# Storing the pieces of the feed-forward way up: another order of differences and stores, and seven staging tiles in place of five

## The chip, the cores and the metric

The kernel runs on one core of a Trainium2 chip. The metric is the device time of one execution in microseconds. It is float32 work throughout; products on TensorE are made from split operands (a high part and the rest, both in the fp32r type).

## The reference, cut to what matters

The whole is one step of a decoder layer: a mixer, a cross-attention over a memory, and a feed-forward part, for 1024 prompt rows and 8 sample rows. The change lies in the feed-forward part alone:

```python
def ffn(x, g, w1, w2):
    h = rmsnorm(x, g) @ w1
    return jnp.square(jax.nn.relu(h)) @ w2
...
    xp = xp + ffn(xp, g_ffn[l], ffn_w1[l], ffn_w2[l])
```

`w1` is 1024 x 4096 and `w2` is 4096 x 1024. Prompt and sample rows stand together as N = 1032 columns of a transposed activation.

## The kernel before, in words

Both feed-forward products are made by a seven-product scheme for 2 x 2 blocks (Strassen's, in Winograd's form). Each matrix is cut into 2 x 2 blocks, seven products of sums and differences of blocks replace eight, and VectorE (DVE) and GpSimd (POOL) make the sums.

**The way up** (`up_unit`, L2049 on) makes the squared-ReLU hidden activation `h`, 256 hidden columns (a *pair*) at a time. There are 16 pairs. The first two (pairs 0 and 1, tiles `hpl`) are made by plain products while the cross-attention ends; the other 14 are *units* 0 to 13, and unit n makes pair n + 2. A unit has eight steps, A11, S2, S1, A12, S3, S4, A21, A22 in this order (i = 0 to 7), and 132 matmuls (a window of one unit also counts the one that crosses its edge): A11, A12 and A22 have 24, the others 12. Their results lie in the banks `fa` to `fg` and `fe`. Three evacuations matter below. ScalarE (ACT) copies the half-made bank `fa` into `gc` after A11, and A12 may only go on adding into `fa` after that (`gc<-fa`). DVE reads the half-made bank `fd` after S3 (`hc<-fd`), and A22 may only go on adding into it after that. Each weight operand of a product is split into a high part (ACT) and a rest (DVE), both named `wop`, five products ahead (`prep`, `LOOK = 5`).

**What is stored.** The way down needs, of each pair, its four blocks and their differences as operands: B11, T1, B22, T3, T2, B21, T4. The four blocks a, b, c, d are the halves (516 columns) of the two `hc` tiles, and `h_done` makes the differences in place: b - a into a's room (T1), d - b into b's (T3), then d - T1 into d's (T2), and c - T2 into c's (T4). Each store (`h_store`, L1952 to L1965) takes a staging tile, writes the high part into it on ACT and the rest on DVE (`halves`), and issues a DMA from SP to the DRAM tensors `hd`. A pair thus has seven stores and four differences: eleven *pieces*. The pieces of pairs 0 and 1 wait in the list `slow`; those of a unit's own pair stand in `early` (put into the program at the start of its step A22) and `rest` (appended to `bg`, taken by `bg_run` in the next unit).

**What sets the order.** The lines of `up_unit` say in which order pieces are emitted, through two tables: how many pieces of `bg` go with each step, and at which steps one of `slow` goes:

```python
            bg_run((2, 1, 1, 3, 1, 0, 0, 0)[i])
            if i in (0, 6) and slow:
                slow.pop(0)()
```

A scheduler then sets each engine's own order from priorities and its idea of when things are ready. Once set, every engine, and SP's list of DMAs too, runs strictly in that order, so an instruction that waits holds up all that stand behind it on its engine.

**Staging tiles.** `ST["ring"]` holds the staging tiles: two halves of `hst`, a part of `wsum`, `MKV`, and from unit 1 a fifth made of two `hst` halves that are stored by two DMAs (L1964). Stores take them in turn. For the last pair only the first two are used, and for the one before it three, because the others' rooms are wanted.

**The way down** follows (`down_unit`): its first operands, B11 and T2 of the first two pairs, are read back into two tiles `hfirst` (`h_load`), whose rooms are taken in the last unit but one (n == 12): one is a `q` slot, one an `e` slot. In the kernel before, the `q` slot that it gets is the one that pair 0's tile `hpl` leaves.

Of the kernel before, what the change touches and what calls it, by code (L numbers as in the profile page):

```python
# [24 lines left out]
N = NP + NS  # L25
# [27 lines left out]
def trunk_step(ctx: ExitStack, tc: tile.TileContext, I: dict, O: list):  # L53
# [17 lines left out]
    def T(tag, w, name, dt=F32):  # L71

        n = SLOTS[tag][1]
        if tag in slots and cur[0] is main:
            pump(lambda: slots[tag])
            assert slots[tag], (tag, name)
            slots[tag].remove(min(slots[tag]))
        return big.tile([128, SLOTS[tag][0]], dt, tag=tag, bufs=n, name=name)[:, :w]

    def v3(ap, a):  # L80
        return ap.rearrange("p (a b) -> p a b", a=a)
# [21 lines left out]
    @contextmanager  # L103
    def lift(n):

        tc.cur_priority -= n
        lifted[0] += n
        yield
        tc.cur_priority += n
        lifted[0] -= n  # L110
# [48 lines left out]
    def act(out, in_, func, **kw):  # L159
        spend("act", 190 + 0.72 * size(in_))  # L160
        if func not in (AF.Ln, AF.Tanh):
            return ACT.activation(out, in_, func, **kw)  # L162
        if func != table["func"]:
            follow(ACT.preload_act_table_set(TABLES[func]).ins)
            table["func"] = func
        ins = ACT.activation(out, in_, func, **kw)
        follow(ins.ins)
        return ins

    def tt(out, a, b, op):  # L170
        spend("dve", 62 + 1.04 * size(out))
        return DVE.tensor_tensor(out, a, b, op=op)  # L172
# [23 lines left out]
    def f32r(ap):  # L196
        return ap.bitcast(F32R)
# [173 lines left out]
    def halves(hi, lo, src):  # L371

        act(hi, src, AF.Copy)
        tt(lo, src, f32(hi), SUB)
# [72 lines left out]
    def bg_run(n):  # L447
        for _ in range(min(n, len(bg))):
            bg.pop(0)()
# [1153 lines left out]
    for tag in "ddee":  # L1603
        p = T(tag, 2048, "x")
# [255 lines left out]
    A11, S2, S1, A12, S3, S4, A21, A22 = range(8)  # L1860
    B11, T2, B21, T1, T3, B22, T4, GA = range(8)
    NPAIR, NPLAIN, NUNIT = DFF // 256, 2, DFF // 512
    HALF, QU, NOP = N // 2, N // 4, 7

    def F(tag, w, name, dt=F32):
        return big.tile([128, SLOTS[tag][0]], dt, tag=tag, bufs=SLOTS[tag][1], name=name)[:, :w]
# [7 lines left out]
    ST, HC, PL = {}, {}, {}  # L1874
# [47 lines left out]
    def prep(q):  # L1922

        if q >= len(QUEUE):
            return
        n, i = QUEUE[q]
        with lift(LIFT_W):
            k = q - BASE[n]
            if k == 0:
                unit_sums(n)  # L1930
            elif k < 5 and n + 1 < len(UNITS):
                unit_raw(n + 1, (k - 1,))
            t = F("wh" if q % 2 else "wl", 1024, "wop", F32R)
            src = SUM[n][i]
            k = src.shape[1]
            hi, lo = v3(t[:, :512], k), v3(t[:, 512:], k)
            halves(hi, lo, src)
            OPS[q] = hi, lo

    def terms(ps, ops, xs, first, last):  # L1940

        n = len(ops)
        for j, ((wh, wl), (xh, xl)) in enumerate(zip(ops, xs)):
            mm(ps, wh, xh, start=first and j == 0, stop=False, skip_group_check=True)
            mm(ps, wh, xl, start=False, stop=False, skip_group_check=True)
            mm(ps, wl, xh, start=False, stop=last and j == n - 1, skip_group_check=True)

    def square_relu(o, x):
        act(o, x, AF.Relu)
        act(o, o, AF.Square)  # L1950

    def h_store(p, op, src):  # L1952

        ring_ = ST["ring"][:{NPAIR - 1: 2, NPAIR - 2: 3}.get(p)]
        st = ring_[ST["n"] % len(ring_)]
        ST["n"] += 1
        hi, lo = (f32r(x) for x in st[:2])
        halves(hi, lo, src)
        d = hd[p // 2].rearrange("(s o) p (q c) -> o p s q c", s=2, q=2)[op, :, :, p % 2]
        if len(st) > 2:  # L1960
            SP.dma_start(d, v3(st[2], 2))
        else:
            for k in range(2):
                SP.dma_start(d[:, k], st[k])  # L1964

    def h_done(p, h):


        def st(op, src):
            return lambda: h_store(p, op, src)  # L1970

        def sub(o, a, b):
            return lambda: tt(o, a, b, SUB)

        a, b, c, d = (x[:, i * HALF:(i + 1) * HALF] for x in h for i in range(2))
        return ([st(B11, a), sub(a, b, a), st(T1, a)],
                [sub(b, d, b), st(T3, b), st(B22, d), sub(d, d, a), st(T2, d), st(B21, c), sub(c, c, d), st(T4, c)])

    def pl_cell(f, g, b):

# [64 lines left out]
    def up_unit(n):  # L2045
        p = UNITS[n][1]
        h = {(f, g): HC["h"][3 * f + g] for f in range(2) for g in range(3)}
        p1, U, V = HC["g"][:3]
        ps = {}  # L2049

        def bank(f, name):
            ps[name] = f(name)[:, :GW]
            return ps[name]

        for i in range(8):
            q = 8 * n + i
            prep(q + LOOK)
            bg_run((2, 1, 1, 3, 1, 0, 0, 0)[i])
            if i in (0, 6) and slow:
                slow.pop(0)()  # L2060
            if i == A22:
                early, rest = h_done(p, HC["t"])
                for fn in early:
                    fn()
            hi, lo = OPS.pop(q)
            w = [(hi[:, k], lo[:, k]) for k in range(4)]
            if i == A11:
                terms(bank(psA, "fa"), w, XOP[B11], True, False)
                with lift(LIFT_E):
                    act(p1, ps["fa"], AF.Copy)  # L2070
                terms(bank(psB, "fe"), w, XOP[GA][:4], True, False)
            elif i == A12:
                terms(ps["fa"], w, XOP[B21], False, True)
                terms(ps["fe"], w, XOP[GA][4:], False, True)
                with lift(LIFT_E):
                    square_relu(h[0, 0], ps["fa"])
                    square_relu(h[0, 2], ps["fe"])
            elif i == S2:
                terms(bank(psD, "fb"), w, XOP[T2], True, True)
                with lift(LIFT_E):  # L2080
                    tt(U, ps["fb"], p1, ADD)
            elif i == S1:
                terms(bank(psD, "fc"), w, XOP[T1], True, True)
                with lift(LIFT_E):
                    tt(V, ps["fc"], U, ADD)
            elif i == S3:
                terms(bank(psC, "fd"), w, XOP[T3], True, False)
                with lift(LIFT_E):
                    tt(h[1, 1], ps["fd"], V, ADD)
                act(h[1, 1], h[1, 1], AF.Relu)  # L2090
                act(h[1, 1], h[1, 1], AF.Square)
            elif i == S4:
                terms(bank(psD, "fg"), w, XOP[B22], True, True)
                with lift(LIFT_E):
                    tt(h[0, 1], ps["fg"], V, ADD)
                act(h[0, 1], h[0, 1], AF.Relu)
                act(h[0, 1], h[0, 1], AF.Square)
            elif i == A21:
                terms(bank(psB, "fe"), w, XOP[GA][:4], True, False)
            else:  # L2100
                terms(ps["fd"], w, XOP[T4], False, True)
                terms(ps["fe"], w, XOP[GA][4:], False, True)
                with lift(LIFT_E):
                    tt(h[1, 0], ps["fd"], U, ADD)
                    square_relu(h[1, 2], ps["fe"])
                act(h[1, 0], h[1, 0], AF.Relu)
                act(h[1, 0], h[1, 0], AF.Square)
            if n == 1 and i == A11:
                ST["ring"].append([F("ws", HALF, "hst") for _ in range(2)])
            if n == NPAIR - NPLAIN - 2:  # L2110

                if i == S2:
                    for op, tag in ((B11, "q"), (T2, "e")):
                        t = F(tag, 2 * N, "hfirst")
                        HOP["r", op] = [v3(t[:, j * N:(j + 1) * N], 2) for j in range(2)]
                elif i in (A12, A21):
                    h_load(0, B11 if i == A12 else T2)
            if n == NPAIR - NPLAIN - 1:

                for op in {S1: (B21, T1), S4: (T3,), A21: (B22,)}.get(i, ()):  # L2120
                    h_load(0, op)
        bg.extend(rest)
# [181 lines left out]
    def w1_blk(f):  # L2304
        return wcols("ffn_w1", [(0, 128 * f, 128)])
# [29 lines left out]
    slow, loads = [], {}  # L2335
# [20 lines left out]
    a, b, c, d, e, f, g = (w1_blk(i) for i in (0, 1, 2, 0, 3, 1, 2))  # L2356
# [28 lines left out]
    for c in range(1, NUNIT):  # L2385
        for op in range(NOP):
            n, k = divmod(2 * op + 1, NOP)
# [44 lines left out]
```

## Time and profile before

| what | us |
|---|---|
| median of 3 runs | 1395.52 |
| lowest of 3 runs | 1391.74 |
| the profiled execution, its own time | 1388.7 |
| its span in the profile | 1387.0 |
| unit 0 of the way up begins | 745.92 |
| the way down begins | 1047.53 |

The span runs from the first to the last instruction of the profile; the 1.7 us between it and the execution's own time lie around it. Engines are PE (TensorE matmuls), DVE (VectorE), ACT (ScalarE), POOL (GpSimd) and SP, whose queue issues the DMAs. A row of the timeline gives start, duration, engine, line, operation, output<-input, and in brackets how long its engine sat idle before it and what ended that. Idle time of an engine that nothing waits for costs nothing.

### The profile page before, as it was taken

Reading aid. Unit: us, or ns where it says so; the run is one execution under the profiler, and the core shown is the slowest. Engines: PE = TensorE matmul, PEld = TensorE weight load, DVE = VectorE, ACT = ScalarE, POOL = GpSimd, SP = SyncE. Lnnn points to the kernel's source line nnn. Section 1 sums busy time; section 2 is a strip of 40 time slices with the busy share of each in tenths; the row PEclk is TensorE's granted clock in tenths of the full one; section 3 lists DMA queues with packets and bytes.
Section 4 is the critical chain, followed back from the end, with each engine's and each line's share of the span. In section 5 each row is a group of like instructions: output and inputs, shape, how many; then the busy total and the mean of one; then the engine's idle time right before and its main releaser. Section 6 shows DMA issues by size and latency. Waiting matters only on the chain.

```text
span 1387.0 us, 24759 instructions
## 1 busy us (share of the span) xinstructions
PE 1320.7 (95%) x9251; PEld 1214.8 (88%) x9251; DVE 1026.6 (74%) x2044; ACT 683.7 (49%) x1399; POOL 263.7 (19%) x245
## 2 busy tenths in 40 slices
PE   6999999999997889998999999999999999999998
PEld 4899888777876877786789999998998999999998
DVE  6276787668767764667699888878877687877785
ACT  5265455245476555555566666756666322222222
POOL 3001011300003101011004322313231333212310
PEclk9999999999999899999899999999999999999999
DMA  6114010211101544442232677776859979776624
GB/s 186 46 49 122 9 49 18 67 25 31 47 9 40 153 131 143 130 140 77 71 123 94 229 255 250 267 255 219 298 200 346 392 271 344 258 244 205 238 72 123
DMA packets 181759, 215.89 MB, mean 156 GB/s; under 512 B 28114, under 2 KB 116238, under 8 KB 181624
## 3 DMA queue, kind: packets, MB, share of 16 engines
q1 hardware_dynamic: 181000, 214.02, 46.4%
q8 instruction: 73, 1.20, 0.4%
q0 software_dynamic: 640, 0.30, 0.1%
q14 instruction: 46, 0.38, 0.1%
HBM read 145.28 MB, written 70.06 MB: 155 GB/s over the span
## 4 chain that ended last, share of the span: by engine, by line
PE 61%; DVE 18%; ACT 9%; DMA 6%; issue 5%; SPq 1%; POOL 0%; DVEq 0%; ACTq 0%; POOLq 0%
PE win L142 9%; PE c L142 7%; PE d L142 7%; PE a L142 6%; PE wo L142 6%; PE b L142 3%; PE v L142 3%; DMA hd<-hst 2%; ACT hc L162 2%; DVE hst L172 2%; DVE hc L172 2%; PE gx L142 2%; PE f L142 2%; DMA hd<-wsum 1%; DVE wop L172 1%
## 5 line engine op out<-in xcount | busy, mean ns | idle before, releaser
L1919 POOL TENSOR_TENSOR wsum<-wraw 128x512 f32<-128x512 f32 x60 | 88.5, 1476 | 402.2 <-DMA wraw<-in_ffn_w_dram 189.2
L142 PE MATMUL win<-XL,wh 128*128 128x344 f32 x384 | 127.4, 332 | 0.0
L142 PE MATMUL win<-XH,wh 128*128 128x344 f32 x384 | 126.8, 330 | 0.2 <-ACT xy L162 0.2
L142 PE MATMUL win<-XH,wl 128*128 128x344 f32 x384 | 126.1, 328 | 0.0
L162 ACT ACTIVATE wh<-ws 128x512 fp32r<-128x512 f32 x130 | 80.0, 627 | 74.6 <-DMA ws<-in_w_out_dram 22.4
L142 PE MATMUL fe<-XH,wop 128*128 128x344 f32 x448 | 114.9, 320 | 0.0
L172 DVE TENSOR_TENSOR wl<-ws,wh 128x512 fp32r<-128x512 f32 x130 | 93.3, 730 | 26.8 <-ACT wh L162 22.1
L162 ACT ACTIVATE wop<-wsum 128x512 fp32r<-128x512 f32 x104 | 65.1, 626 | 97.3 <-PE d L142 29.1
L162 ACT ACTIVATE wop<-wraw 128x512 fp32r<-128x512 f32 x104 | 64.1, 625 | 93.2 <-PE a L142 30.4
L172 DVE TENSOR_TENSOR wop<-wsum,wop 128x512 fp32r<-128x512 f32 x104 | 88.0, 847 | 25.8 <-ACT wop L162 25.4
L172 DVE TENSOR_TENSOR wop<-wraw,wop 128x512 fp32r<-128x512 f32 x104 | 75.9, 729 | 14.1 <-ACT wop L162 13.2
L142 PEld LDWEIGHTS fe<-XH,wop 128*128 128x128 f32 x448 | 78.9, 188 | 0.0
L142 PEld LDWEIGHTS win<-XL,wh 128*128 128x128 f32 x384 | 72.7, 189 | 5.2 <-issue 3.9
L142 PEld LDWEIGHTS win<-XH,wl 128*128 128x128 f32 x384 | 72.8, 190 | 3.6 <-issue 2.7
L142 PEld LDWEIGHTS win<-XH,wh 128*128 128x128 f32 x384 | 72.8, 190 | 3.3 <-issue 1.9
L142 PE MATMUL fe<-XL,wop 128*128 128x344 f32 x224 | 71.5, 319 | 0.0
L142 PE MATMUL d<-XH,wop 128*128 128x258 f32 x352 | 67.3, 283 | 0.0
L172 DVE TENSOR_TENSOR hst<-hc,hst 128x516 fp32r<-128x516 f32 x63 | 55.7, 891 | 15.6 <-ACT hst L162 15.3
L142 PE MATMUL wo<-XH,wh 128*128 128x344 f32 x192 | 64.3, 335 | 2.0 <-ACT wh L162 2.0
L142 PE MATMUL wo<-XH,wl 128*128 128x344 f32 x192 | 64.2, 334 | 1.0 <-DVE wl L172 0.9
L162 ACT ACTIVATE hc<-hc 128x344 f32<-128x344 f32 x126 | 61.1, 485 | 4.9 <-DVE hc L172 3.2
L162 ACT ACTIVATE hst<-hc 128x516 fp32r<-128x516 f32 x63 | 39.6, 634 | 48.1 <-DVE hc L172 35.5
(551 smaller groups left out, 4143.4 us busy)
## 6 DMA issues: line engine op xcount, KB each, us to landing
wraw<-in_ffn_w_dram SPq DMA_DIRECT2D x120, 256.0 KB
hd<-hst SPq DMA_DIRECT2D x52, 516.0 KB
XH<-hd SPq DMA_DIRECT2D x34, 516.0 KB
XL<-hd SPq DMA_DIRECT2D x34, 516.0 KB
hd<-wsum SPq DMA_DIRECT2D x23, 516.0 KB
xoph<-hd SPq DMA_DIRECT2D x20, 516.0 KB
xopl<-hd SPq DMA_DIRECT2D x20, 516.0 KB
hd<-MKV SPq DMA_DIRECT2D x19, 516.0 KB
```

The lines of the kernel that those rows point to most:

```text
L142: PE.matmul(out, lhsT, rhs, start=start, stop=stop, **kw)
L162: return ACT.activation(out, in_, func, **kw)
L172: return DVE.tensor_tensor(out, a, b, op=op)
L1919: POOL.tensor_tensor(o, a, b, op=op)
```

## The change

It edits four places.

- `h_done`: the store of T1 goes from `early` to `rest`, behind the difference d - b; T3's store goes behind the difference that makes T2. The pieces of a pair are the same eleven.
- `up_unit`: with step A11 three pieces of `bg` are emitted in place of two, and the pieces of `slow` go with steps A21 and A22 (i = 6, 7) in place of A11 and A21 (0, 6).
- `up_unit`: at unit 6's step A11 two more staging tiles are added, the halves of one `q` slot.
- `h_store`: pair 13 uses the first five staging tiles only, so that the new ones are free for `hfirst`.

```diff
@@ h_store @@
-        ring_ = ST["ring"][:{NPAIR - 1: 2, NPAIR - 2: 3}.get(p)]
+        ring_ = ST["ring"][:{NPAIR - 1: 2, NPAIR - 2: 3, NPAIR - 3: 5}.get(p)]
@@ h_done @@
-        return ([st(B11, a), sub(a, b, a), st(T1, a)],
-                [sub(b, d, b), st(T3, b), st(B22, d), sub(d, d, a), st(T2, d), st(B21, c), sub(c, c, d), st(T4, c)])
+        return ([st(B11, a), sub(a, b, a)],
+                [sub(b, d, b), st(T1, a), st(B22, d), sub(d, d, a), st(T3, b), st(T2, d), st(B21, c), sub(c, c, d), st(T4, c)])
@@ up_unit @@
-            bg_run((2, 1, 1, 3, 1, 0, 0, 0)[i])
-            if i in (0, 6) and slow:
+            bg_run((3, 1, 1, 3, 1, 0, 0, 0)[i])
+            if i in (6, 7) and slow:
                 slow.pop(0)()
@@ up_unit @@
             if n == 1 and i == A11:
                 ST["ring"].append([F("ws", HALF, "hst") for _ in range(2)])
+            if n == 6 and i == A11:
+
+                t = F("q", 2 * N, "hst")
+                ST["ring"] += [(x[:, :HALF], x[:, HALF:], x) for x in (t[:, :N], t[:, N:])]
```

TensorE's own order does not change. Two places of the other engines' orders are shown.

The first is ACT in unit 7 of the way up, from the evacuation of `fe` after A12 to the first evacuation of A22's results. `hpl` is a plain pair's tile; `hc_7328` holds blocks a and b, `hc_7329` c and d; rows that write `hst`, `wsum_7330` or `MKV` from `hc` or `hpl` are the high parts of stores. Before:

```order
L162 ACTIVATE hc_7328<-fe_8955 128x344
L162 ACTIVATE wop_9050<-wsum_7330 128x512
L162 ACTIVATE hc_7328<-hc_7328 128x344
L162 ACTIVATE wop_9073<-wsum_7330 128x512
L162 ACTIVATE hc_7329<-hc_7329 128x344 x2
L162 ACTIVATE wsum_7330<-hpl_6855 128x516
L162 ACTIVATE wop_9093<-wraw_7212 128x512
L162 ACTIVATE hc_7328<-hc_7328 128x344 x2
L162 ACTIVATE hst_7647<-hc_7328 128x516
L162 ACTIVATE wop_9113<-wsum_7330 128x512
L162 ACTIVATE hst_7331<-hc_7328 128x516
L162 ACTIVATE hc_7329<-hc_7329 128x344 x2
```

The same stretch in the changed kernel, from the evacuation of S3's bank on:

```order
L162 ACTIVATE hc_7329<-hc_7329 128x344 x2
L162 ACTIVATE wop_9092<-wraw_7212 128x512
L162 ACTIVATE hc_7328<-hc_7328 128x344 x2
L162 ACTIVATE MKV_124<-hc_7328 128x516
L162 ACTIVATE wop_9112<-wsum_7330 128x512
L162 ACTIVATE hst_7644<-hc_7328 128x516
L162 ACTIVATE hc_7329<-hc_7329 128x344 x2
```

and, right behind it, up to the next unit's `gc<-fa`:

```order
L162 ACTIVATE hst_7331<-hc_7329 128x516
L162 ACTIVATE hc_7329<-fe_9098 128x344
L162 ACTIVATE wop_9151<-wsum_7330 128x512
L162 ACTIVATE hc_7329<-hc_7329 128x344
L162 ACTIVATE MKV_124<-hpl_6855 128x516
L162 ACTIVATE gc_6996<-fa_9162 128x344
```

The plain pair's store has gone from between the evacuations of S3 and S4 (one stands just ahead of `gc<-fa` now). The store of T1 (`hst_7331<-hc_7328` before, `hst_7644<-hc_7328` now) has kept its place between the `wop` and the evacuation of A22.

The second place is SP's list of DMAs around `hfirst`, the room that the way down's first B11 is read into (hd0 holds pairs 0 and 1, hd3 pairs 6 and 7, hd6 pairs 12 and 13). Before, in unit 5:

```order
L1961 DMA hd0_4481<-wsum_7330 128x2x516
L1961 DMA hd3_4484<-hst_7331 128x2x516
L2139 DMA hfirst_10084<-hd0_4481 128x1032
L1961 DMA hd3_4484<-MKV_124 128x2x516
L1961 DMA hd3_4484<-hst_7331 128x2x516
```

Now, in unit 11:

```order
L1908 DMA wraw_7366<-in_ffn_w1_dram 128x2x256 x3
L1961 DMA hd6_4487<-hst_8749 128x2x516
L2143 DMA hfirst_10081<-hd0_4481 128x1032 x2
L1961 DMA hd6_4487<-hst_7331 128x2x516
L1961 DMA hd6_4487<-wsum_7330 128x2x516
```

The two loads have moved six units later and stand right behind the last store out of the new staging tiles (`hst_8749`), whose slot they fill.

## Rows read from the trace of the kernel before

**Rows 1.** The page: busy time of each engine, its share of the span, instructions.

```profile
PE 1320.7 (95%) x9251; PEld 1214.8 (88%) x9251; DVE 1026.6 (74%) x2044; ACT 683.7 (49%) x1399; POOL 263.7 (19%) x245
```

**Rows 2.** Windows, units 3, 4, 5, 8, 9, 10, 13, way down's start: length, busy times, clock, DMA.

```profile
808.26:829.04 20.78, 20.78 (x133) 20.78 (x133) 16.87 (x24) 14.43 (x29) 5.96 (x5) 1.00 0.76 259
829.04:850.57 21.53, 21.12 (x134) 20.75 (x134) 18.00 (x25) 13.24 (x27) 6.05 (x5) 1.00 0.66 237
850.57:873.22 22.65, 21.33 (x133) 20.72 (x133) 19.80 (x29) 15.63 (x32) 5.97 (x4) 1.00 0.80 276
...
914.78:937.97 23.19, 21.28 (x133) 20.74 (x133) 19.18 (x28) 14.61 (x30) 6.18 (x4) 1.00 0.67 236
937.97:962.18 24.21, 21.40 (x134) 20.71 (x133) 20.14 (x29) 16.30 (x33) 6.24 (x4) 1.00 0.66 234
962.18:983.56 21.38, 21.03 (x133) 20.77 (x133) 17.54 (x25) 14.28 (x29) 7.70 (x5) 1.00 0.75 259
...
1025.12:1047.53 22.41, 21.30 (x133) 20.76 (x133) 18.03 (x26) 13.62 (x28) 6.68 (x4) 1.00 0.70 246
1047.53:1061.73 14.20, 12.23 (x100) 11.82 (x99) 11.39 (x12) 8.83 (x19) 6.20 (x4) 1.00 0.97 358
```

**Rows 3.** Timeline of PE: its longer idle stretches in units 5, 8 and 9.

```profile
869.36 0.40 PE L142 MATMUL fd<-XH,wop 128*128 128x344 f32 x1 [1.23 <-DVE hc L172]
...
923.99 0.42 PE L142 MATMUL fa<-XH,wop 128*128 128x344 f32 x1 [1.50 <-ACT gc L162]
...
946.78 0.42 PE L142 MATMUL fa<-XH,wop 128*128 128x344 f32 x1 [1.11 <-ACT gc L162]
...
958.32 0.40 PE L142 MATMUL fd<-XH,wop 128*128 128x344 f32 x1 [1.70 <-DVE hc L172]
```

**Rows 4.** Timeline of ACT: stores that waited, and two evacuations of `fa`.

```profile
866.18 0.64 ACT L162 ACTIVATE hst<-hc 128x516 fp32r<-128x516 f32 x1 [1.81 <-DMA hd<-hst]
...
904.51 0.64 ACT L162 ACTIVATE wsum<-hc 128x516 fp32r<-128x516 f32 x1
...
913.53 0.64 ACT L162 ACTIVATE wsum<-hpl 128x516 fp32r<-128x516 f32 x1 [3.12 <-DMA hd<-wsum]
...
920.15 0.64 ACT L162 ACTIVATE hst<-hc 128x516 fp32r<-128x516 f32 x1 [3.36 <-DVE hc L172]
...
923.50 0.44 ACT L162 ACTIVATE gc<-fa 128x344 f32<-128x344 f32 x1
...
935.17 0.64 ACT L162 ACTIVATE hst<-hpl 128x516 fp32r<-128x516 f32 x1 [1.97 <-DMA hd<-hst]
...
954.66 0.64 ACT L162 ACTIVATE hst<-hc 128x516 fp32r<-128x516 f32 x1 [2.41 <-DMA hd<-hst]
...
976.02 0.64 ACT L162 ACTIVATE MKV<-hpl 128x516 fp32r<-128x516 f32 x1 [1.70 <-DMA hd<-MKV]
...
1006.53 0.64 ACT L162 ACTIVATE wsum<-hc 128x516 fp32r<-128x516 f32 x1 [3.64 <-DVE hc L172]
...
1032.40 0.44 ACT L162 ACTIVATE gc<-fa 128x344 f32<-128x344 f32 x1
```

**Rows 5.** Timeline of DVE in unit 8's beginning.

```profile
914.20 0.69 DVE L172 TENSOR_TENSOR wsum<-hpl,wsum 128x516 fp32r<-128x516 f32 x1 [3.81 <-ACT wsum L162]
914.82 1.78 DVE L172 TENSOR_TENSOR wop<-wraw,wop 128x512 fp32r<-128x512 f32 x1
...
919.43 0.68 DVE L172 TENSOR_TENSOR hc<-hc 128x516 f32<-128x516 f32 x1
```

**Rows 6.** ACT's waits from 740 to 1070 us: in total, times, longest.

```profile
ACT hst L162 <- DVE hc L172: 35.3, 25, 3.6
...
ACT hst L162 <- DMA hd<-hst: 17.2, 13, 2.5
```

**Rows 7.** Chain that ended last: a store, from its issue to its landing.

```profile
909.05 4.46 DMA hd<-wsum
```

**Rows 8.** Timeline of SP's queue in unit 5.

```profile
859.05 0.33 SPq L2139 DMA_DIRECT2D hfirst<-hd  x1
```

## The prediction

> **What bounds the kernel now.** I read the page's first lines, then windows of one unit each, then the timelines of PE, ACT and DVE around PE's idle stretches, then ACT's waits. TensorE is busy for 1320.7 us [rows 1] of the span's 1387.0, so only its gaps can be won, and the change touches those of the way up and the hand-over to the way down alone.
>
> The reader is to see in the windows that a unit without a gap takes 20.78 us and PE is busy throughout (unit 3 [rows 2]). Eight of the 14 units are of that kind. The other six last 21.53, 22.65, 23.19, 24.21, 21.38 and 22.41 us [rows 2], so they are over the floor by 0.75 (unit 4), 1.87 (5), 2.41 (8), 3.43 (9), 0.60 (10) and 1.63 us (13): 10.69 us together. The way down's first window is 14.20 us with 12.23 us of PE, which is 1.97 us more. The clock is 1.00 in all of them. So 12.66 us is all that this change can win: 0.9% of the time.
>
> PE's named releasers are ACT's `gc<-fa` and DVE's `hc<-fd` [rows 3]. Neither is slow in itself; both engines stand in order behind a store that waits for its staging tile. Unit 8 shows the chain. ACT waits 3.12 us at 913.53 for the DMA that still reads the tile `wsum`, to put a plain pair's piece in it [rows 4]. DVE, whose next row is the rest of that piece, stands for 3.81 us; then its next `wop` takes 1.78 us, and the difference b - a starts at 919.43 only [rows 5]. ACT has meanwhile gone on to T1's store and waits 3.36 us for this difference until 920.15; `gc<-fa` starts at 923.50 [rows 4], and PE, which wanted that bank, stands 1.50 us before 923.99 [rows 3]. In unit 9 the plain pair's store at 935.17 (1.97 us of waiting, just before the unit) leads to the 1.11 us at 946.78 and T4's store at 954.66 (2.41 us) to the 1.70 us at 958.32; in unit 5 T4's store at 866.18 (1.81 us) leads to 1.23 us [rows 3, 4].
>
> ACT waits for store DMAs 17.2 us on `hst` alone, and for differences on DVE 35.3 us there [rows 6]. The second figure is larger, but most of it comes with no gap of PE: in unit 12, for one, T1's store waits 3.64 us at 1006.53 [rows 4], and the unit keeps the floor.
>
> **The change part by part.**
>
> *Two more staging tiles.* Fourteen pairs' seven stores and 14 of the plain pairs are 112, or 8 a unit. With five tiles a tile's turn comes every 5/8 of 20.78 us, or 13.0 us; with seven, 18.2 us. What a tile needs shows on `wsum`: written at 904.51, issued at 909.05, landed 4.46 us later, free at 913.53: 9.0 us [rows 4, 7]. Five tiles leave 4.0 us for bunching, and the pieces are bunched; seven leave 9.2 us. So I take the DMA waits of units 7 to 12 as gone: 3.12, 1.97, 2.41 and 1.70 us of ACT [rows 4], and the gaps behind them. Of unit 8's 2.41 I count 2.0 (the 0.4 left comes from a difference), of unit 9's 3.43 all, of unit 10's all 0.6 (its wait is the one at 976.02): 6.0 us. The bounds are 0 and 6.44.
>
> *The plain pairs' pieces at A21 and A22.* ACT's order shows what this does: the store that stood between the evacuations of S3 and S4, where A22 waits for DVE, now stands ahead of `gc<-fa`. That helps units 4 and 5, where there are still five tiles. Unit 4's gap follows such a store; I count 0.4 of its 0.75. In unit 5 the two loads into `hfirst`, the first of them at 859.05 [rows 8], also leave for unit 11. I count half of its 1.87, or 0.9. The bounds for the two units are 0 and 2.62.
> It costs something in front of `gc<-fa`: one store of 0.64 us [rows 4] more in the units that get one there. In unit 13, where T1's wait was long, `gc<-fa` started at 1032.40 [rows 4], 7.28 us after the unit's start; PE wants the bank after 48 of 132 matmuls, 7.56 us. So the room is 0.3 us in a late unit, and some 0.3 us is lost in each of perhaps three units: 1.0 us, with bounds of 0 and 2.
>
> *T1 behind another difference.* The order says that this does little on ACT: T1's store stands where it stood, straight behind the next `wop` and ahead of A22's evacuation. The 3.36 us kind of wait stays. B22's store, which needs no difference, now comes ahead of T3's, so T3's wait shrinks; neither ended a gap by itself, so I count 0, with bounds of -1 and +1. As many instructions run as before; the work hides below PE's, as DVE is busy for 16.87 to 20.14 us of a unit [rows 2].
>
> *Five to seven, and back.* Where the count changes at unit 6, the fifth tile gets T1 and, two stores later, T3 of the same pair: 2/8 of 20.78 is 5.2 us, against 9.0 needed: up to 3.8 us of ACT. A wait of 2.41 us made a gap of 1.70 and one of 1.81 a gap of 1.23 [rows 3, 4], so a gap is about 0.6 to 0.7 shorter than the wait, and this one at most 3.1 us. But the tile is stored by two DMAs, one for each half, and only the high one holds ACT, so I take 0.3.
>
> *The loads into `hfirst` in unit 11.* Their slot comes free when the last store out of the new tiles lands, and SP stands for those 4.46 us [rows 7] with all its list. Behind the loads stand the next pair's stores, which A22 starts, some 8 us on; so it is hidden, and the loads have about 50 us until the way down. Without that cover the stores are 4.5 us late, and PE would lose up to 3.8 us by the measure above. Unit 13 and the hand-over still have two or three tiles: 0 of their 3.60 us.
>
> Sum: 6.0 + 0.4 + 0.9 - 1.0 - 0.3 = 6.0 us won. The profiled execution took 1388.7 us (span 1387.0 and 1.7 around it), so it would be 1382.7. It lies 6.8 below the shown median of 1395.52 and 3.0 below the lowest, 1391.74; the mean of these three is 1392.0, and I set the forecast 6.0 below that: 1386.0 us.
>
> **The rivals.**
>
> *A: the waits only change their name.* With the tiles free, ACT still waits for differences, twice as long in total [rows 6], and T1's place is kept. For it speaks that every gap's last link is a difference or an evacuation that came late. Against it: unit 12 with such a wait alone has no gap, and each chain above begins at a DMA. Won: about 1 us, so 1391.
>
> *B: slower, by DVE beside POOL.* With A11 three pieces now stand where two stood, at the time when POOL makes its sums. A DVE operation beside these takes 1.78 us where its like takes 0.69 [rows 5]: 1.1 us more. DVE's busy time is 18.5 us in the mean of the seven whole units of rows 2, so two more such operations a unit would fill it to 20.7 and from the third on DVE sets the unit: 21.8 us. Fourteen units are then 305.3 us, where they are 301.6 now (1047.53 - 745.92): 3.7 us slower, or 1396. Against it: POOL is busy only for some 6 us of a unit, four operations, and in unit 8 several meet DVE already; one moved piece hardly adds three.
> The Trainium skill, SBUF — State Buffer (SBUF: two separate sides), has a rule for this: a DVE operation with two inputs in SBUF and a GpSimd operation that reads SBUF use one shared port pair, and the second waits for all of the first. The trace agrees that far (1.78 against 0.69 us); by the rule every meeting costs that, which is this rival's price.
>
> *C: all is won.* The hand-over and unit 13 profit too, through earlier differences: 12.66 us less, 1379. Against it: their staging is not touched.
>
> **How the numbers follow.** Forecast 0.60, A 0.22, B 0.12, C 0.06. A measurement of this kernel can tell about 2%, 28 us, from no change. No case gets there on either side: the most that can be won is 12.66 us, and B costs 3.7. So 0.98 for within 2%, and 0.01 on each side for what I have not seen. The range takes in C's end with 1 us beyond, 1378, and B's 1396; executions of one kernel here lie 6.8 us apart, which this covers too.
>
> **What would show it.** Right: in the profile after, units 8 to 10 at 20.8 to 21.3 us; no ACT wait on `hd` stores over 1 us in units 7 to 11; T1's waits of 2 to 3.6 us still there; `hfirst` loads in unit 11. Wrong: DMA waits gone and units 8 and 9 still over 22 us (A); all units longer, with DVE over 20 us in each (B); a new gap of over 2 us in unit 6, or in 11 and 12 behind SP's wait (the two terms that I put near nothing).

## The result, and the profile after

The changed kernel takes 1383.08 us (median of 8 runs, 1380.99 to 1384.58); the kernel before, measured beside it, takes 1390.74 (median of 8 runs, 1387.22 to 1395.52 and one of 1615.16, without which the median is 1389.73). The ratio is 0.9945 with a 95% interval of 0.9933 to 0.9958: 7.65 us less by these medians, 6.65 without that one run. By the bound of 2% that is no change, though the interval lies wholly below 1. The forecast was 1386.0, and 6.0 us less.

The page of the changed kernel, first the engines' busy time (it answers to [rows 1]). The execution on this page took 1383.71 us, with a span of 1382.0:

```profile
PE 1322.5 (96%) x9251; PEld 1218.7 (88%) x9251; DVE 1026.2 (74%) x2044; ACT 684.2 (50%) x1399; POOL 263.3 (19%) x245
```

Windows of units 4, 5, 7, 8, 9, 10, 11 and 13 and of the way down's start, with the columns of [rows 2]: length, busy time of PE, PEld, DVE, ACT and POOL, granted clock, DMA share, GB/s.

```profile
830.38:851.16 20.78, 20.78 (x134) 20.78 (x133) 18.25 (x28) 14.29 (x29) 4.58 (x4) 1.00 0.72 254
851.16:872.19 21.03, 21.03 (x134) 20.77 (x133) 18.22 (x27) 15.15 (x30) 7.83 (x6) 1.00 0.77 267
...
892.97:914.62 21.65, 21.02 (x134) 20.76 (x133) 19.14 (x28) 14.80 (x30) 5.54 (x4) 1.00 0.75 265
914.62:935.40 20.78, 20.78 (x134) 20.78 (x133) 18.48 (x27) 14.39 (x29) 6.32 (x5) 1.00 0.76 266
935.40:956.18 20.78, 20.78 (x134) 20.78 (x133) 18.36 (x27) 14.81 (x30) 6.58 (x4) 1.00 0.77 271
956.18:976.96 20.78, 20.78 (x134) 20.78 (x133) 18.41 (x27) 14.39 (x29) 6.46 (x5) 1.00 0.77 269
976.96:997.74 20.78, 20.78 (x134) 20.78 (x133) 17.64 (x24) 13.98 (x28) 8.82 (x6) 1.00 0.79 274
...
1018.52:1043.25 24.73, 22.59 (x133) 22.31 (x133) 19.11 (x26) 14.47 (x29) 6.34 (x4) 0.93 0.66 233
1043.25:1057.45 14.20, 12.68 (x103) 12.30 (x103) 12.41 (x13) 9.74 (x20) 6.50 (x4) 1.00 1.01 358
```

Units 4, 8, 9 and 10 are on the floor of 20.78 us, unit 5 nearly; together they give back 8.8 us. Unit 7 pays 0.87 and unit 13, which was 1.63 over, is 3.95 over. The way up as a whole lasts 295.99 us (1043.25 - 747.26) where it lasted 301.61: 5.07 us over 14 floors in place of 10.69. That is 5.62 us less; the spans of the two profiled executions differ by 5.0, so not all of the 7.65 shows in them. The way down's first window has 0.45 us more of PE.

The timeline of PE after has two longer stretches of idle time in the way up, one in unit 7 and one in unit 13; the four of [rows 3] are gone:

```profile
910.76 0.40 PE L142 MATMUL fd<-XH,wop 128*128 128x344 f32 x1 [0.63 <-DVE hc L172]
...
1028.36 0.43 PE L142 MATMUL fa<-XH,wop 128*128 128x344 f32 x1 [2.14 <-ACT gc L162]
```

ACT's timeline after, to compare with [rows 4]: T1's stores of units 7 and 12, the one store that waited over 1 us for a DMA between unit 7 and unit 12's end, and unit 13's chain.

```profile
895.85 0.64 ACT L162 ACTIVATE wsum<-hc 128x516 fp32r<-128x516 f32 x1 [3.63 <-DVE hc L172]
...
999.32 0.64 ACT L162 ACTIVATE wsum<-hc 128x516 fp32r<-128x516 f32 x1 [3.35 <-DVE hc L172]
...
1003.56 0.64 ACT L162 ACTIVATE hst<-hc 128x516 fp32r<-128x516 f32 x1 [1.45 <-DMA hd<-hst]
...
1018.62 0.64 ACT L162 ACTIVATE wsum<-hc 128x516 fp32r<-128x516 f32 x1 [3.73 <-DMA hd<-wsum]
...
1024.52 0.64 ACT L162 ACTIVATE hst<-hc 128x516 fp32r<-128x516 f32 x1 [4.74 <-DVE hc L172]
...
1027.87 0.44 ACT L162 ACTIVATE gc<-fa 128x344 f32<-128x344 f32 x1
```

DVE in unit 13 after (as [rows 5] showed it for unit 8):

```profile
1019.30 1.78 DVE L172 TENSOR_TENSOR wsum<-hc,wsum 128x516 fp32r<-128x516 f32 x1 [4.58 <-ACT wsum L162]
1021.00 1.78 DVE L172 TENSOR_TENSOR wop<-wsum,wop 128x512 fp32r<-128x512 f32 x1
1022.70 1.78 DVE L172 TENSOR_TENSOR hc<-hc 128x516 f32<-128x516 f32 x1
1024.40 0.50 DVE L172 TENSOR_TENSOR hc<-fd,gc 128x344 f32<-128x344 f32 x1
```

This is unit 8's old chain in a new place. The last pair but one stores its B11 into the part of `wsum` that the T4 of the pair before has just filled (the ring of three tiles begins at the index where the ring of five ended). ACT stands 3.73 us for that DMA, DVE stands 4.58 us behind ACT and then makes three operations of 1.78 us each, T1's store waits 4.74 us for the third of them, and `gc<-fa` comes at 1027.87, 2.14 us too late. In the kernel before the same store waited less, and its rest on DVE was short (the rows of ACT and DVE, and PE's one longer gap of that unit):

```profile
1024.25 0.64 ACT L162 ACTIVATE wsum<-hc 128x516 fp32r<-128x516 f32 x1 [2.47 <-DMA hd<-wsum]
...
1024.91 0.70 DVE L172 TENSOR_TENSOR wsum<-hc,wsum 128x516 fp32r<-128x516 f32 x1 [3.32 <-ACT wsum L162]
...
1043.67 0.40 PE L142 MATMUL fd<-XH,wop 128*128 128x344 f32 x1 [1.04 <-DVE hc L172]
```

There `gc<-fa` came 7.28 us after the unit's start and PE did not wait for it; now it comes 9.35 us after. Of these 2.07 us, 0.98 are the store that starts later and 1.08 the rest on DVE that takes 1.78 us in place of 0.70. The gap of 1.04 us further on is gone.

SP's queue after, in units 11 and 13: the two loads into `hfirst`, and the T4 store that unit 13 waits for.

```profile
996.35 0.81 SPq L2143 DMA_DIRECT2D hfirst<-hd  x2
...
1011.80 0.42 SPq L1961 DMA_DIRECT2D hd<-wsum  x1
```

The waits of ACT from 740 to 1070 us after (reason, sum, times, longest), which answer to [rows 6]:

```profile
ACT hst L162 <- DVE hc L172: 40.1, 25, 4.7
...
ACT hst L162 <- DMA hd<-hst: 10.7, 9, 2.4
```

So the waits for differences have grown and the gaps are gone: the total of a wait says little here. A group that says more is that of the plain pairs' 14 stores. Groups of ACT's instructions by shape, 740 to 1070 us (count, busy, mean ns, then the idle time just ahead of them and what ended it), of the kernel before:

```profile
L162 ACT ACTIVATE hst<-hpl 128x516 fp32r<-128x516 f32 x7 | 4.4, 635 | 5.5 <-DMA hd<-hst 5.4
L162 ACT ACTIVATE wsum<-hpl 128x516 fp32r<-128x516 f32 x5 | 3.2, 636 | 7.7 <-DMA hd<-wsum 7.7
...
L162 ACT ACTIVATE MKV<-hpl 128x516 fp32r<-128x516 f32 x2 | 1.3, 636 | 1.8 <-DMA hd<-MKV 1.7
```

and of the changed kernel:

```profile
L162 ACT ACTIVATE hst<-hpl 128x516 fp32r<-128x516 f32 x9 | 5.6, 627 | 3.2 <-DMA hd<-hst 3.2
L162 ACT ACTIVATE MKV<-hpl 128x516 fp32r<-128x516 f32 x3 | 1.9, 632 | 0.2
...
L162 ACT ACTIVATE wsum<-hpl 128x516 fp32r<-128x516 f32 x2 | 1.2, 624 | 0.0
```

The 14 plain stores stood still for 15.0 us before (5.5 + 7.7 + 1.8) and for 3.4 us now. What the experiments had to settle is which of the edits did that.

### The profile page after: what moved, and what is told of

It reads as the page before. It is cut to its first block, busy times and chain, and to the rows that moved or that the text cites. A ratio compares the mean times of both kernels' runs of the same rounds, so it can differ in the third digit from the quotient of the medians.

```text
span 1382.0 us, 24764 instructions
## 1 busy us (share of the span) xinstructions
PE 1322.5 (96%) x9251; PEld 1218.7 (88%) x9251; DVE 1026.2 (74%) x2044; ACT 684.2 (50%) x1399; POOL 263.3 (19%) x245
## 4 chain that ended last, share of the span: by engine, by line
PE 66%; DVE 15%; ACT 6%; DMA 5%; issue 4%; SPq 1%; POOL 0%; DVEq 0%; ACTq 0%; POOLq 0%
PE win L142 9%; PE c L142 7%; PE d L142 7%; PE a L142 6%; PE wo L142 6%; PE b L142 3%; PE v L142 3%; DMA hd<-hst 3%; PE f L142 2%; PE fe L142 2%; PE gx L142 2%; DVE hc L172 2%; DVE hst L172 2%; PE wq L142 2%; PE wmo L142 2%
## 5 line engine op out<-in xcount | busy, mean ns | idle before, releaser
L172 DVE TENSOR_TENSOR wop<-wsum,wop 128x512 fp32r<-128x512 f32 x104 | 91.7, 883 | 23.4 <-ACT wop L162 19.1
L162 ACT ACTIVATE hst<-hc 128x516 fp32r<-128x516 f32 x67 | 42.5, 635 | 48.6 <-DVE hc L172 40.1
```

## The experiments

The edits have three parts: *tiles* (two more staging tiles from unit 6 on, and the limit of five for pair 13), *steps* (the plain pairs' pieces at steps 6 and 7 in place of 0 and 6), and *order* (T1's and T3's stores behind other differences, with the new table of pieces). The loads into `hfirst` follow from the tiles. All times below are medians against the kernel before on the same chip.

**Tiles alone** (the kernel before with this):

```diff
-        ring_ = ST["ring"][:{NPAIR - 1: 2, NPAIR - 2: 3}.get(p)]
+        ring_ = ST["ring"][:{NPAIR - 1: 2, NPAIR - 2: 3, NPAIR - 3: 5}.get(p)]
...
+            if n == 6 and i == A11:
+                t = F("q", 2 * N, "hst")
+                ST["ring"] += [(x[:, :HALF], x[:, HALF:], x) for x in (t[:, :N], t[:, N:])]
```

> The two more staging tiles alone, with the old order of pieces and the old steps for the plain pairs' pieces. Theory (the tiles free the DMA waits of units 7 to 10, and these were the gaps): units 8 to 10 at 20.8 to 21.3 us, units 4 and 5 still about 0.7 and 1.9 us over, 5 to 6 us faster than the kernel before (1385 where it takes 1391). Rival (the new steps of the plain pairs' pieces did it): units 8 and 9 still over 22 us, at most 2 us faster.

Measured: 1391.49 against 1388.38 us, ratio 1.0015 [1.0000, 1.0031]. The theory of the prediction falls: the term of 6.0 us is nothing, or a loss. The gaps changed their place: units 9 and 10 are 0.3 and 0.2 us over the floor, but units 6, 8 and 12 are 2.9, 4.1 and 1.4 over. The timeline of ACT, SP's queue, DVE and PE in this kernel, from unit 7's end into unit 8:

```profile
905.93 0.64 ACT L162 ACTIVATE hst<-hc 128x516 fp32r<-128x516 f32 x1 [2.45 <-DVE hc L172]
906.96 0.64 ACT L162 ACTIVATE hst<-hc 128x516 fp32r<-128x516 f32 x1 [0.39 <-DVE hc L172]
...
908.16 0.36 SPq L1961 DMA_DIRECT2D hd<-hst  x1
...
913.53 0.64 ACT L162 ACTIVATE hst<-hpl 128x516 fp32r<-128x516 f32 x1 [3.30 <-DMA hd<-hst]
...
914.20 0.70 DVE L172 TENSOR_TENSOR hst<-hpl,hst 128x516 fp32r<-128x516 f32 x1 [3.20 <-ACT hst L162]
...
924.73 0.45 ACT L162 ACTIVATE gc<-fa 128x344 f32<-128x344 f32 x1
...
925.23 0.43 PE L142 MATMUL fa<-XH,wop 128*128 128x344 f32 x1 [2.32 <-ACT gc L162]
```

With seven tiles a plain store waits as long as it did with five. The order of ACT in this kernel tells why (rows of stores alone, with the pieces' names and times added; `hst_8749` holds the two new tiles, `hst_7331` the first two):

```
L162 ACTIVATE hst_8749<-hc_7329 128x516      T2 of pair 8, into the second new tile (905.93)
L162 ACTIVATE hst_7331<-hc_7329 128x516      T4 of pair 8 (906.96)
L162 ACTIVATE hst_8749<-hpl_6855 128x516     plain pair's B22, into the same tile again (913.53)
L162 ACTIVATE MKV_124<-hc_7328 128x516       B11 of pair 9
L162 ACTIVATE hst_7647<-hc_7328 128x516      T1 of pair 9
```

The tiles are dealt in the order in which the pieces are emitted, and there six stores lie between T2 of pair 8 and this plain store. But a plain store needs nothing of the unit, so the scheduler has put it ahead of three of those six (B11, T1 and T3 of pair 9); two others (B21 of pair 8 and another plain store) had run before T2. One store is left in between, 7.6 us pass from fill to fill, and the DMA issued at 908.16 has not landed. Unit 6's gap of 2.22 us begins at such a store as well: ACT waits 3.05 us at 871.39. More tiles didn't cure that here: what counts is how many stores really run between two uses of a tile.

**The change without the tiles**: both `h_store` and the block at unit 6 as before, steps and order as after.

> The changed kernel without the two tiles: new order of T1 and T3, new steps of the plain pairs' pieces, five tiles to the end. Theory (tiles): units 8 to 10 keep 4 of their 6.4 us over the floor, 1 to 3 us faster than the kernel before. Rival (the steps): units 8 to 10 near the floor, 5 us or more faster; unit 13 tells beside it whether its longer gap comes with the order (it stays at 24 to 25 us) or with the later loads into hfirst (it falls to about 22.4).

Measured: 1383.79 us, ratio 0.9967 [0.9951, 0.9984]. The gain lies between the theory's 1 to 3 us and the rival's 5: its greater part is there without the tiles. Units 4, 5, 8 and 10 are within 0.2 us of the floor; unit 9 is 3.84 over. Unit 13 is 0.95 over, so its longer gap in the changed kernel does not come with steps and order alone.

**Steps alone**:

```diff
-            if i in (0, 6) and slow:
+            if i in (6, 7) and slow:
```

> The kernel before with the plain pairs' pieces at steps A21 and A22 and nothing else. Theory (tiles): 0 to 2 us faster, units 4 and 5 nearer to the floor, unit 8 or 9 still over 22 us. Rival (the steps): 4 us or more faster, no unit but 13 over 21.5 us.

Measured: 1382.55 us, ratio 0.9954 [0.9935, 0.9973]: one pair of numbers carries nearly all of the gain, and the rival is right in the time. The plain stores wait 7.6 us in place of 15.0, and no plain store stands between S3's evacuation and A22's any more. The way up is 4.76 over its floors, of which unit 9 has 3.83: there the rival, who wanted no unit but 13 over 21.5 us, missed. Its window:

```profile
932.75:957.36 24.61, 22.55 (x134) 22.30 (x133) 20.66 (x28) 14.79 (x30) 8.40 (x6) 0.93 0.70 242
```

and the gap of PE in it, by the timeline:

```profile
951.96 0.40 PE L142 MATMUL fd<-XH,wop 128*128 128x344 f32 x1 [2.06 <-DVE hc L172]
```

A plain store is ahead of it again, now before S3's evacuation: ACT waits 1.91 us for its tile at 948.69.

**Unit 13's store in another tile** (the changed kernel with this):

```diff
+        if (p, op) == (NPAIR - 2, B11):
+            st = ST["ring"][3]
+        else:
             st = ring_[ST["n"] % len(ring_)]
             ST["n"] += 1
```

> The changed kernel with one store moved to another tile: B11 of pair 14 goes into MKV, which has been free since unit 12's start, and not into the part of wsum that T4 of pair 13 has left 5.7 us before. Theory (unit 13's gap of 2.14 us begins at that store's wait of 3.73 us, and the fall of the clock behind it goes with it): unit 13 at 20.8 to 22 us in place of 24.7, the kernel 2 to 4 us faster than the changed one, so about 1380. Rival (the hand-over has too few tiles whichever is taken, so the wait goes to the next store): unit 13 over 23.5 us, within 1 us of the changed kernel.

Measured: 1381.34 us, ratio 0.9938 [0.9917, 0.9959]. Unit 13 falls from 3.95 to 0.36 us over the floor: its gap is the wait for that one tile. In the median it is 1.7 us better than the changed kernel (2 to 4 were expected), with intervals that overlap.

**The change without the new order** (tiles and steps):

> The kernel before with the two tiles and the new steps (A21, A22) of the plain pairs' pieces, but with T1's store and the table of pieces as they were. Theory (the steps bring the gain, the order of T1 and T3 nothing): ratio to before 0.993 to 0.996, units 8 to 10 within 0.5 us of 20.78, unit 13 again with a gap of about 2 us. Rival (the order of T1 and T3 is worth 2 us or more beside the other two): ratio 0.997 or above.

Measured: 1381.08 us, ratio 0.9936 [0.9916, 0.9957], the theory's range. Units 8 to 10 are within 0.13 us. Unit 13 is 1.99 over, with two gaps of 0.55 and 0.92 us rather than one of 2: a miss in the form.

**The plain pairs' pieces at A12 and S3**, on the kernel before:

```diff
-            if i in (0, 6) and slow:
+            if i in (3, 4) and slow:
```

> The kernel before with the plain pairs' pieces at steps A12 and S3 (3, 4) in place of A11 and A21 (0, 6); nothing else. In ACT's order no plain store then stands between S4's evacuation and A22's, just as with (6, 7). Theory (what costs is a plain store at that place, since its wait for a DMA delays the difference and the half-made banks): about the gain of the steps (6, 7), ratio 0.994 to 0.997, no gap of over 1 us in units 4, 5 and 8. Rival (A21 and A22 are special, or the gain of e3 came by chance of which tile is free): ratio 0.999 to 1.003, with two or more gaps in units 4 to 10.

Measured: 1382.5 against 1390.61 us, ratio 0.9948 [0.9929, 0.9967], the same as A21 and A22. Units 4 and 8 are on the floor and unit 5 is 0.24 over it; unit 9 has a gap of 2.18, here behind a store of the unit's own pair that waits 2.63 us for its tile at 947.75. The steps 6 and 7 are nothing special.

**The plain pairs' pieces at A11 and S2**, on the kernel before (`(0, 1)` in that line):

> The kernel before with the plain pairs' pieces at steps A11 and S2 (0, 1) in place of A11 and A21 (0, 6); nothing else. In ACT's order a plain store then stands between S4's evacuation and A22's in nearly every unit. Theory (the place costs): slower than before, ratio 1.001 to 1.006, with gaps of 1 to 2.3 us in three or more of the units 4 to 10. Rival (the place does not matter): ratio 0.995 to 1.000, two gaps or fewer.

Measured: 1395.04 us, ratio 1.0037 [1.0021, 1.0053]: slower than before, as the theory wanted. The way up is 17.4 us over its floors, with gaps of over 1 us in units 4, 5, 7 and 9. Unit 7 of this kernel on ACT, DVE and PE:

```profile
901.87 0.64 ACT L162 ACTIVATE hst<-hpl 128x516 fp32r<-128x516 f32 x1 [3.89 <-DMA hd<-hst]
...
902.53 1.28 DVE L172 TENSOR_TENSOR hst<-hpl,hst 128x516 fp32r<-128x516 f32 x1 [4.21 <-ACT hst L162]
...
909.70 0.42 PE L142 MATMUL fa<-XH,wop 128*128 128x344 f32 x1 [1.96 <-ACT gc L162]
```

The plain store stands between the two ACT operations of S4's evacuation, ahead of A22's, and waits 3.89 us; DVE stands with it for 4.21, so A22's evacuation, the difference, T1's store and `gc<-fa` all come late.

**The changed kernel once more**, beside these three:

> The changed kernel once more, unchanged, beside the others on one chip. Ratio to before 0.9933 to 0.9958 as it was; unit 13 with its gap of about 2.1 us and a fall of the clock behind it.

Measured: 1382.26 us, ratio 0.9947 [0.9926, 0.9967]; unit 13 with a gap of 2.27 us, 4.07 over the floor. The result repeats.

**The change with the old steps** (tiles and order):

> The changed kernel with only the steps of the plain pairs' pieces put back to A11 and A21 (0, 6). In ACT's order a plain store stands again between S4's evacuation and A22's in about half of the units 4 to 10. Theory (the steps carry the gain, tiles and order do nothing without them): ratio to before 0.998 to 1.003, and gaps in two or more of the units 4 to 10. Rival (tiles and order help each other): ratio 0.997 or below, no gap of over 1 us in units 8 to 10.

Measured: 1391.24 against 1390.22 us, ratio 1.0012 [0.9997, 1.0028]. Without the steps the other edits together bring nothing; units 4 and 9 have gaps of 2.74 and 2.29 us, and the plain stores wait 13.2.

**Order alone** (`h_done` and the table of pieces):

> The kernel before with the new place of T1's and T3's stores and the new table of pieces alone. Theory: 0 from this edit, ratio 0.998 to 1.003 (the prediction's bounds of -1 and +1 us are 0.9993 to 1.0007). Rival (the order is worth something that the tiles hide): ratio 0.997 or below.

Measured: 1391.68 us, ratio 1.0013 [0.9999, 1.0027]. Nothing, or a small loss.

**Steps, tiles, and unit 13's store** (the order of T1 and T3 as before):

> The kernel before with the new steps, the two tiles, and the B11 of pair 14 stored through MKV (the tile at index 3, whose store is older) in place of the tile whose turn it is; the order of T1 and T3 as before. Theory: nothing is left in units 0 to 12 but under 1.5 us together, and unit 13 loses its wait for the tile: ratio to before 0.991 to 0.994, the fastest of all. Rival (unit 13's gap comes from the differences and only changes its place): ratio 0.994 to 0.996, unit 13 over the floor by 2 us or more.

Measured: 1379.15 us, ratio 0.9926 [0.9899, 0.9952]: the fastest of all in the median, 11 us under the kernel before, though its interval overlaps those of the other kernels with new steps. The way up is 1.11 us over 14 floors. Units 8, 9, 12 and 13 of it:

```profile
914.86:935.64 20.78, 20.78 (x134) 20.78 (x134) 18.81 (x27) 14.39 (x29) 6.26 (x4) 1.00 0.76 269
935.64:956.42 20.78, 20.78 (x134) 20.77 (x134) 19.01 (x26) 14.81 (x30) 6.24 (x4) 1.00 0.73 252
...
997.98:1018.93 20.95, 20.95 (x134) 20.76 (x133) 16.75 (x27) 14.30 (x30) 3.95 (x3) 1.00 0.88 297
1018.93:1040.65 21.72, 21.03 (x134) 20.77 (x133) 17.46 (x22) 12.79 (x27) 6.34 (x4) 1.00 0.70 252
```

**The two tiles for the plain stores alone**, steps and order as before:

```diff
-        st = ring_[ST["n"] % len(ring_)]
-        ST["n"] += 1
+        if p < NPLAIN and ST["own"]:
+            st = ST["own"][0]
+            ST["own"] = ST["own"][::-1]
+        else:
+            st = ring_[ST["n"] % len(ring_)]
+            ST["n"] += 1
...
+            if n == 6 and i == A11:
+                t = F("q", 2 * N, "hst")
+                ST["own"] = [(x[:, :HALF], x[:, HALF:], x) for x in (t[:, :N], t[:, N:])]
```

> The kernel before with the two new tiles from unit 6 on, but for the plain pairs' stores alone; steps and order as before. The scheduler then puts the last six plain stores into units 6 and 7, each with a tile whose last store lies three stores or more back (one of them only some 7 us, which should wait about 2 us); units 8 to 10 have none. Theory (the loss is the plain stores' wait for a tile that was filled just before, so seven tiles in common don't help and two of their own do): plain stores wait under 9 us in all in place of 15.0, units 8 to 10 within 0.6 us of the floor, units 4 and 5 as before (about 0.8 and 1.7 over), ratio to before 0.995 to 0.998. Rival (only the new steps help, as a store costs at its place without a wait too): ratio 0.999 to 1.003, gaps of over 1 us in units 6 and 7.

Measured: 1386.6 against 1389.63 us, ratio 0.9978 [0.9963, 0.9992]. The same two tiles that bring nothing in the common ring bring 3 us here. The groups of the plain stores:

```profile
L162 ACT ACTIVATE hst<-hpl 128x516 fp32r<-128x516 f32 x10 | 6.3, 631 | 4.0 <-DMA hd<-hst 3.7
L162 ACT ACTIVATE wsum<-hpl 128x516 fp32r<-128x516 f32 x4 | 2.5, 636 | 3.7 <-DMA hd<-wsum 3.5
```

and the windows of units 5 and 9:

```profile
851.93:877.47 25.54, 22.82 (x133) 22.27 (x133) 24.01 (x36) 17.55 (x35) 6.05 (x5) 0.93 0.77 272
...
939.90:960.68 20.78, 20.78 (x133) 20.78 (x133) 17.45 (x27) 15.16 (x31) 6.50 (x5) 1.00 0.67 234
```

The plain stores wait 7.7 us, and units 7 to 13 are all on the floor, as the theory has it. But no plain store runs in these units any more (the last six run in units 5 and 6), so they don't tell a store that waits from one that merely stands there. What the theory missed: the scheduler, with nothing to hold the pieces back, put some of them as early as unit 5, where DVE now works for 24.01 us, more than a unit, and PE loses 4.76.

The traces of all these kernels together tell the two apart. In them 29 plain stores stand between S3's evacuation and A22's. Eighteen of them waited 1.71 us or less; behind sixteen of these PE's next wait at `fa` is 0.5 us or less, and the other two follow a plain store that had just waited 1.97 and 3.35 us. One of the sixteen, at the end of unit 5 of the kernel with steps, tiles and unit 13's store, where unit 6 keeps the floor:

```profile
872.75 0.64 ACT L162 ACTIVATE hst<-hpl 128x516 fp32r<-128x516 f32 x1 [1.32 <-DMA hd<-hst]
```

Eight waited 2.40 us or more, and behind six of them PE waits 1.50 to 2.74 us at `fa`, behind two not at all. So at `fa` it is the wait that costs, and a store that merely stands there costs little.

Side by side (plain: the time that the 14 plain stores stood, summed from the groups as above; over: the way up over 14 floors of 20.78 us):

| kernel | steps | tiles | order | plain, us | over, us | ratio |
|---|---|---|---|---|---|---|
| before | 0, 6 | | | 15.0 | 10.69 | 1 |
| tiles alone | 0, 6 | yes | | 14.1 | 12.70 | 1.0015 |
| order alone | 0, 6 | | yes | 17.5 | 14.42 | 1.0013 |
| tiles, order | 0, 6 | yes | yes | 13.2 | 14.44 | 1.0012 |
| at A11 and S2 | 0, 1 | | | 13.8 | 17.40 | 1.0037 |
| own tiles | 0, 6 | own | | 7.7 | 4.95 | 0.9978 |
| steps alone | 6, 7 | | | 7.6 | 4.76 | 0.9954 |
| at A12 and S3 | 3, 4 | | | 5.0 | 4.71 | 0.9948 |
| steps, order | 6, 7 | | yes | 8.1 | 4.88 | 0.9967 |
| steps, tiles | 6, 7 | yes | | 5.2 | 3.16 | 0.9936 |
| after | 6, 7 | yes | yes | 3.4 | 5.07 | 0.9945 |
| after, once more | 6, 7 | yes | yes | 3.8 | 5.20 | 0.9947 |
| after, unit 13's store | 6, 7 | yes | yes | 3.8 | 2.46 | 0.9938 |
| steps, tiles, unit 13's store | 6, 7 | yes | | 4.6 | 1.11 | 0.9926 |

Plain and over are of one execution each; the changed kernel's two executions differ by 0.4 and 0.13 us in them. The ratio is worked out over all runs and is not just that of the two medians. The two halves of the table don't mix: where the plain stores stand for 13 us or more, nothing is won; where they stand for 8.1 or less, 3 to 11 us are. Within a half the total of the waits does not order the kernels (13.8 us of it go with 17.40 over, 15.0 with 10.69): where a store stands counts beside how long it waits.

## Why the prediction was right, and where it was wrong

*The bound and the total: right.* Only PE's gaps on the way up were to be won. The forecast lies 2.9 us above the time, its gain of 6.0 us 1.7 below the measured 7.65 (the base, 1392.0, is 1.3 above the median), and the time stands inside the range. That the sum came out is luck: its one large term, 6.0 us, is nothing by itself, and the three small ones that the new steps were given, 0.3 us in all, stand for some 6.

*Two more staging tiles, 6.0 us: wrong.* Alone they bring nothing. The step that failed is "With five tiles a tile's turn comes every 5/8 of 20.78 us, or 13.0 us; with seven, 18.2 us". That holds for stores that run in the order in which they are dealt. The rows of before spoke against it already: `wsum` was written at 904.51 and wanted again at 910.41 (913.53 less the 3.12 us of waiting [rows 4]), 5.9 us later, where a turn was said to be 13.0. I took the difference for bunching that seven tiles would cover; it was a plain store out of its turn, with a single store (`MKV`, at 905.76) between. Beside the new steps the tiles take unit 9's 3.83 us away; over against steps alone the way up is 1.60 us shorter with them (4.76 and 3.16), while the two ratios (0.9954 and 0.9936) have intervals that overlap.

*The plain pairs' pieces, 0.4 + 0.9 - 1.0 us: the mechanism named, the size wrong.* The prediction saw that the store between the evacuations of S3 and S4 would go, but counted it for units 4 and 5 alone, since it held that the tiles would have settled units 8 to 10. Alone it is worth 5.8 us by the medians and 6.4 by the ratio, and it clears nearly all of units 4, 5, 8 and 10. The price of 1.0 us in front of `gc<-fa` did not appear: no gap at `fa` is left in units 0 to 12 of the changed kernel. (The room of 0.3 us was misread as well: it runs to the start of the copy, which takes 0.44 us [rows 4].)

*T1 behind another difference, 0 with bounds of -1 and +1.* About right, or a small loss: alone it gives 1.0013 [0.9999, 1.0027]. In all four pairs of the table that differ by the order alone the way up is longer with it, by 3.73, 1.74, 1.91 and 0.12 us, but no interval of the times shows it. T1's waits are still there (3.63 and 3.35 us), with no gap behind them.

*Five to seven, 0.3 us; `hfirst` in unit 11, 0.* Right: unit 6 is on the floor, the loads stand at 996.35, and unit 11 takes 20.78 us.

*Unit 13, 0 of its 1.63: wrong, by 2.3 us.* "Unit 13 and the hand-over still have two or three tiles" looked at the number of tiles and not at which one is dealt; moving that one store gives the 2.3 us back and more. The table's kernels tell which edits bring the loss: with the new steps unit 13 is 0.9 us over without the tiles, 1.99 with them, and 3.95 with tiles and order together. Why the T4 store that it waits for takes longer to land (some 6.8 us from its issue, where it took 5.1 before) was not tried; unit 12 moves 276 GB/s where the kernel before moved 224.

*What was to show it.* Units 8 to 10 at 20.78, no wait over 1 us for a store's DMA in units 7 to 11, T1's waits as before: all seen, and all of it was seen of the sum of the edits. None of these signs could tell the tiles from the steps, which is why the split stayed wrong with a right total.

*The rivals.* A falls: the waits for differences did grow on `hst` (40.1 from 35.3 us), but the gaps went. B falls for this change, as DVE's windows stay at 17 to 19 us. Its longer operations do have a part in unit 13's loss, the 1.08 us above: the three of 1.78 us stand beside POOL's sums, which run there from 1019.22 to 1025.64. The Trainium skill's rule on the shared port pair (SBUF — State Buffer, SBUF: two separate sides), by which one of the two engines waits for the whole of the other's operation, fits them. A unit that DVE fills came elsewhere, but by the number of pieces: with own tiles DVE was busy 24.01 us in unit 5 with 36 operations, only two of them of some 1.78 us, and that unit lost 4.76. C falls: unit 13 lost, and the hand-over kept 1.52 us of its 1.97.

## What to carry to other kernels

A ring of buffers gives the slack that its length says only if stores run in the order in which buffers are dealt. Where a scheduler may move work that depends on nothing near it, look up how many stores truly run between two uses of one buffer, and either emit such work where it will run (here one pair of numbers, some 6 us) or give it buffers of its own; adding buffers to the common ring can bring nothing. When several edits are costed together, find for each a sign in the profile that it alone would leave.

## What the runs showed that was not expected

An idle stretch of PE can cost nearly twice its length. After unit 13's 2.14 us without a matmul the granted clock was at its lower level for a part of the next 5.4 us. Windows of the changed kernel from the end of the gap on:

```profile
1028.36:1030.80 2.44, 2.44 (x13) 2.44 (x14) 2.31 (x4) 1.74 (x4) 0.00 (x0) 0.81 0.49 186
1030.80:1033.80 3.00, 3.00 (x14) 3.00 (x12) 2.02 (x5) 1.37 (x3) 0.00 (x0) 0.58 1.00 273
1033.80:1036.80 3.00, 3.00 (x22) 3.00 (x21) 2.81 (x5) 1.65 (x4) 0.00 (x0) 1.00 0.92 328
```

A clock of 1.00 is 2.4 GHz here; 0.58 is mostly 1.2 GHz, and 14 matmuls fit where 22 do after it. The unit lost 3.95 us: 2.14 of gap and 1.81 of slower matmuls (PE busy 22.59 for 20.78). The same fall follows the 2.06 us of steps alone in unit 9, the 1.96 us of A11 and S2 in unit 7, and the 2.23 us of own tiles in unit 5. The length of the gap alone does not decide: after the 2.32 us of tiles alone in unit 8 the window's clock is 1.00, and so it is in the windows of [rows 2], where gaps reach 1.70 us [rows 3]. In the way up of all these runs ten gaps of 1.96 to 2.74 us had such a fall behind them; three, of 2.22, 2.32 and 2.45 us, had not, and neither had any shorter one. The prediction priced gaps by their length only.
